# A hybrid decoder layer on one core: the opening's norm weight, the order at the stage entries, and the place of the mLSTM gates

## The chip, the cores and the metric

The kernel runs on one core of a Trainium2 chip, as one launch. The core has a matrix engine (PE; PEld in the profile is its weight load), a vector engine (DVE), a scalar engine (ACT), GpSimd (POOL) and a sync engine (SP) that here only issues DMAs. Each engine works through its own queue in order and waits on semaphores; 16 DMA engines move data between HBM and SBUF. The metric is the device time of one execution in microseconds (us), the median of several runs.

## What is computed

One layer, for 512 tokens of 1024 float32 values: a half-step SwiGLU FFN, a mixer, and a second half-step FFN, each with a norm before and a norm after it.

```python
f = swiglu(rmsnorm(x, ffn1_pre_g[l]), ffn1_w_gate[l], ffn1_w_up[l], ffn1_w_down[l])
x = x + 0.5 * rmsnorm(f, ffn1_post_g[l])
y = hybrid_mixer(rmsnorm(x, mix_pre_g[l]), positions, w_in[l], ...)
x = x + rmsnorm(y, mix_post_g[l])
f = swiglu(rmsnorm(x, ffn2_pre_g[l]), ffn2_w_gate[l], ffn2_w_up[l], ffn2_w_down[l])
x = x + 0.5 * rmsnorm(f, ffn2_post_g[l])
```

`rmsnorm(x, g)` is `x * rsqrt(mean(x*x) + 1e-6) * g`. The mixer joins dilated attention (four heads, three groups each) with an mLSTM of four heads. The mLSTM's gates are, per head and token, `ig = i_pre + i_bias` and `lf = log_sigmoid(f_pre + f_bias)`; running sums of `lf` and a running maximum over them scale its keys and values.

## The kernel before

**Numbers.** Every float32 operand of a projection is split into a rounded high part and the rest, the low part (names with `h` and `l`). A product is three matmuls: high·high, high weight with low activation, and low weight with high activation. ACT makes the high part (a copy into the rounded type), DVE the low part (a subtraction).

**Tiling.** Tokens stand in four tiles of 128 (`xs[0]` to `xs[3]`, D = 1024 values a row). After a norm a tile is turned by eight PE transposes (`turn_norm`) into `hTh` and `hTl`, which hold the model dimension on partitions in eight chunks `k` (KD = 8). Weights come as 512 KB tiles of 128 x 1024 through `load_w` (L79): SP issues the DMA, ACT casts (L86), DVE subtracts (L88).

**Order.** The framework orders each engine's instructions by a planner, which goes by program order and by its own estimate of when each is ready; it may draw a later instruction ahead of one that it takes to be late. `tc.issue_after(i)` ties an instruction behind `i` on its engine. The class `Order` (L243) uses it to write an engine's order out by hand: each of its instructions stands behind the one before. PSUM has eight banks, handed out in turn.

**The opening** (L640 to L661). PE runs 28 matmuls on zeros (L71, `WARM`) while nothing else is there. SP issues x tile 0, then the norm weight `ffn1_pre_g` broadcast to all 128 partitions (`gain`, L91), x tile 1, two weight tiles (gate and up of block f = 0), and x tiles 2 and 3. `prenorm_first` (L134) squares a tile with its row sums on ACT (L138), adds EPS on DVE (L139), takes the power −0.5 on POOL (L100), and multiplies x, the row's factor and the gain in two halves on DVE (L142). Tiles 0 and 1 are turned at once; turning tiles 2 and 3 is put into the list `todo`.

**Stage entries.** `by_halves` (L181) starts a stage before all tokens are ready: first half the tokens (tiles 0 and 1), then the other half, for two groups of two outputs (`b` = 0 and 1, in FFN 1 gate and up). In each group three terms `i` run over both outputs, eight matmuls of 256 columns for each: `i` = 0 high·high, 1 high weight with `hTl`, 2 low weight with `hTh`. After (n, i) = (0, 2) and (1, 0) of the first half one entry of `todo` is run, which turns tile 2 and tile 3. The function is used at three places: FFN 1, the mixer (its first four q/k projections, L899) and FFN 2. At the two later places the weights after the first are cast behind `pins`, the turning of the tiles before.

**FFN rest.** `token_parts` (L251) forms sums of the token halves on DVE and ACT for the later blocks, in a part of `aT`, the tile that receives the FFN's hidden values.

**Mixer.** Attention goes head by head (L954 to L965): q/k projections (`qk_proj`), the exchange of softmax statistics between groups (`exchange`, small steps on DVE and ACT, ending in L841), the transposes of the weights (`turn`, L850), the values. `v12_proj` projects the values of two heads at a time and sends them through DRAM on POOL's queue. `gates()` (L920) turns the gates' pre-activations, applies biases and the logarithm on ACT, and forms two scans and their sums on DVE; `gates_turn` (L940) turns the results for later use by the mLSTM. `gates()` stands behind `scores(0)`, and `gates_turn` in the round of head 1. The mLSTM reads the results only after head 3. The row of the head norm, `hg`, is fetched by POOL into a buffer that `gates()` uses, so it waits for it.

## Time and profile before

| what | value |
|---|---|
| median of 3 runs | 1358.43 us (1358.39 to 1358.49) |
| the profiled execution | 1358.6 us, its span 1356.8 us |
| mean granted PE clock over the span | 0.998 |
| DVE, ACT, POOL busy | 71%, 44%, 2% of the span |
| HBM read and written | 144.63 MB and 4.19 MB, 110 GB/s over the span |

The span runs from the first to the last instruction that the profiler saw; the execution's time has a little more around it. A row of the timeline gives start and duration in us, the engine, the line of the kernel, the operation, what it writes and reads, and the count of instructions merged; in brackets stands how long the engine was idle before it and what ended that. A matmul's duration is longer than the distance to the next start, since they are pipelined. A row of the windows view gives a stretch, its length, the busy time of PE, PEld, DVE, ACT and POOL (each with its count of instructions), PE's granted clock, the share of time in which the 16 DMA engines were busy, and GB/s.

### The profile page before, as it was taken

The page shows a single profiled execution, that of the slowest core. Times are in us where ns is not written, and L with a number is a line of the kernel's source. Part 1 is how long each engine was busy: PE and PEld are TensorE (multiplying, and loading weights), DVE is VectorE, ACT ScalarE, POOL GpSimd, SP SyncE. Part 2 cuts the span into 40 slices and gives each one's busy share as a digit, 9 for nine tenths or more (in the row PEclk, how much of TensorE's full clock was granted, in tenths as well). Part 3 has the DMA queues.
Part 4 walks back from the last instruction along what each step waited for, and adds up shares of the span by engine and source line. Part 5 has one row for each costly group of instructions (what it writes and reads, how often), then busy time and mean ns, then how long its engine had stood idle before and what let it go on. Part 6 is the DMA issues. An engine that isn't in the chain of part 4 may idle for free.

```text
span 1356.8 us, 19908 instructions
## 1 busy us (share of the span) xinstructions
PE 1342.3 (99%) x7976; PEld 1192.8 (88%) x7976; DVE 967.8 (71%) x1482; ACT 601.7 (44%) x969; POOL 32.8 (2%) x56
## 2 busy tenths in 40 slices
PE   8999999999999999999999999999999999999998
PEld 8899999878898888888888888888889999998786
DVE  7799898996772885775756754334378798997983
ACT  5444444554633532445535443222264444444552
POOL 1000000000200000000000000000010000000000
PEclk9999999999999999999999999999999999999999
DMA  5233333654233422422222232233213333335541
GB/s 202 93 109 103 106 104 109 232 174 152 66 95 118 140 82 89 144 74 78 78 78 78 79 117 73 102 97 109 93 46 111 94 97 107 108 106 196 173 148 62
DMA packets 41661, 150.11 MB, mean 111 GB/s; under 512 B 4716, under 2 KB 4716, under 8 KB 41312
## 3 DMA queue, kind: packets, MB, share of 16 engines
q1 hardware_dynamic: 39600, 141.08, 31.7%
q0 software_dynamic: 1968, 7.76, 1.8%
q8 instruction: 62, 1.02, 0.3%
q14 instruction: 31, 0.25, 0.1%
HBM read 144.63 MB, written 4.19 MB: 110 GB/s over the span
## 4 chain that ended last, share of the span: by engine, by line
PE 89%; DVE 6%; ACT 2%; issue 2%; DMA 1%; SPq 0%; DVEq 0%; POOLq 0%; ACTq 0%
PE p L178 11%; PE qb_b L321 9%; PE qb_a L321 9%; PE pq L178 8%; PE pm L178 6%; PE qa_a L321 4%; PE qa_b L321 4%; PE acc_o L229 3%; PE pvo L997 2%; PE pvo L999 2%; PE pvo L998 2%; PE pg_a L188 2%; PE pg_b L188 2%; PE pq L188 2%; PE pg_b L178 2%; PE pg_a L178 2%
## 5 line engine op out<-in xcount | busy, mean ns | idle before, releaser
L178 PE MATMUL pq<-hTh_mx,wh_qk 128*128 128x512 f32 x160 | 63.2, 395 | 0.0
L178 PE MATMUL pq<-hTl_mx,wh_qk 128*128 128x512 f32 x160 | 62.4, 390 | 0.0
L88 DVE TENSOR_TENSOR wl_qk<-wf_qk,wh_qk 128x1024 fp32r<-128x1024 f32 x24 | 29.3, 1220 | 40.2 <-ACT wh_qk L86 29.9
L178 PE MATMUL pm<-hTh_mx,wh_mqk 128*128 128x512 f32 x128 | 50.3, 393 | 0.0
L997 PE MATMUL pvo<-wh_vo,hTh_mx 128*128 128x512 f32 x128 | 50.2, 392 | 0.0
L178 PE MATMUL pm<-hTl_mx,wh_mqk 128*128 128x512 f32 x128 | 49.9, 390 | 0.0
L178 PE MATMUL p<-hTh_mx,wh_gm 128*128 128x512 f32 x128 | 49.9, 390 | 0.0
L999 PE MATMUL pvo<-wl_vo,hTh_mx 128*128 128x512 f32 x128 | 49.8, 389 | 0.0
L178 PE MATMUL p<-hTl_mx,wh_gm 128*128 128x512 f32 x128 | 49.8, 389 | 0.0
L998 PE MATMUL pvo<-wh_vo,hTl_mx 128*128 128x512 f32 x128 | 49.8, 389 | 0.0
L86 ACT CAST wh_qk<-wf_qk 128x1024 fp32r<-128x1024 f32 x24 | 25.0, 1045 | 54.1 <-PE pw L741 27.3
L1150 DVE SCALAR_TENSOR_TENSOR t<-t,p 128x512 f32<-128x512 f32 x16 | 11.0, 688 | 42.7 <-PE p L178 42.7
L88 DVE TENSOR_TENSOR wl_mqk<-wf_mqk,wh_mqk 128x1024 fp32r<-128x1024 f32 x16 | 19.6, 1222 | 29.7 <-ACT wh_mqk L86 25.3
L178 PE MATMUL pq<-hTh_mx,wl_qk 128*128 128x512 f32 x160 | 39.6, 389 | 0.0
L888 DVE SCALAR_TENSOR_TENSOR z<-pm,cw,z 128x511 f32<-128x511 f32 (+2 forms) x48 | 35.2, 742 | 1.4 <-ACT z L886 0.9
L249 ACT CAST wh_a<-cd_a 128x1024 fp32r<-128x1024 f32 x18 | 18.9, 1049 | 39.0 <-DVE cd_a L249 39.0
L321 PE MATMUL qa_a<-hTl_f,wh_a 128*128 128x256 f32 x144 | 36.1, 283 | 0.0
L321 PE MATMUL qa_b<-hTl_f,wh_b 128*128 128x256 f32 x144 | 36.1, 283 | 0.0
L321 PE MATMUL qa_a<-hTh_f,wh_a 128*128 128x256 f32 x144 | 36.1, 283 | 0.0
L321 PE MATMUL qa_b<-hTh_f,wh_b 128*128 128x256 f32 x144 | 36.1, 283 | 0.0
L249 ACT CAST wh_b<-cd_b 128x1024 fp32r<-128x1024 f32 x18 | 18.9, 1049 | 37.9 <-DVE cd_b L249 37.9
L178 PEld LDWEIGHTS pq<-hTh_mx,wl_qk 128*128 128x128 f32 x160 | 30.0, 188 | 6.2
(679 smaller groups left out, 4396.3 us busy)
## 6 DMA issues: line engine op xcount, KB each, us to landing
wf_qk<-in_wqk SPq DMA_DIRECT2D x24, 512.0 KB, 3.6
B_a<-in_wdq SPq DMA_DIRECT2D x21, 512.0 KB, 3.8
B_b<-in_wdq SPq DMA_DIRECT2D x21, 512.0 KB, 4.4
g_a<-in_wgu SPq DMA_DIRECT2D x18, 512.0 KB, 3.7
u_a<-in_wgu SPq DMA_DIRECT2D x18, 512.0 KB, 3.8
g_b<-in_wgu SPq DMA_DIRECT2D x18, 512.0 KB, 3.8
u_b<-in_wgu SPq DMA_DIRECT2D x18, 512.0 KB, 3.8
wf_mqk<-in_wmqk SPq DMA_DIRECT2D x16, 512.0 KB, 3.3
```

The lines of the kernel that those rows point to most:

```text
L86: nc.scalar.copy(wh, wf)
L88: nc.vector.tensor_tensor(wl, wf, wh.bitcast(F32), op=ALU.subtract)
L178: nc.tensor.matmul(out, lhsT=wt[:, k * P:(k + 1) * P], rhs=x[:, k, tok], start=n == 0, stop=n == len(terms) - 1)
L188: nc.tensor.matmul(outs[b][:, tok], lhsT=ws_[b][w][:, k * P:(k + 1) * P], rhs=x[:, k, tok], start=i + k + hf == 0, stop=hf == 1 and i == 2 ...
L229: nc.tensor.matmul(out, lhsT=x[:, tk], rhs=w[:, cs], start=first and n == 0, stop=last and n == 2, skip_group_check=True)
L249: self.last[eng] = getattr(getattr(nc, eng), fn)(*args, **kw).ins
L321: nc.tensor.matmul(out, lhsT=wt[:, i * P:(i + 1) * P], rhs=y[:, i, :], start=first and n == 0, stop=last and n == len(terms) - 1, skip_gro ...
L888: nc.vector.scalar_tensor_tensor(z[:, s:], src[:, :T - s], cw[:, ct, 3 - s:4 - s], z[:, s:], op0=ALU.mult, op1=ALU.add)
L997: nc.tensor.matmul(out, lhsT=hTh[:, k, tk], rhs=wh[:, cs], start=k == 0, stop=False)
L998: nc.tensor.matmul(out, lhsT=hTl[:, k, tk], rhs=wh[:, cs], start=False, stop=False)
L999: nc.tensor.matmul(out, lhsT=hTh[:, k, tk], rhs=wl[:, cs], start=False, stop=k == KD - 1)
L1150: nc.vector.scalar_tensor_tensor(t1[:, b, :], t1[:, b, :], 1.0, p2[b], op0=ALU.add, op1=ALU.mult)
```

## The change

1. The row `ffn1_pre_g` is fetched four times, to partitions 0, 32, 64 and 96 of a tile that DVE has set to zero, by DMAs of 4 KB on ACT's queue; two stream shuffles spread each over its 32 partitions. The broadcast on SP's queue goes.
2. The first weights are loaded into a part of `aT` that is not yet in use (`raw`), before x tiles 2 and 3, and not into buffers of `wf`.
3. The opening's ACT and DVE instructions have a written order (`Order`); tile 1's EPS step stands between the two halves of tile 0's scaling, and tiles 2 and 3 are scaled between and behind the low halves of the first weights. `token_parts` is tied behind the last of them on DVE.
4. The matmuls on zeros are 32 at the start, 8 behind the turning of tile 0, and 5 behind that of tile 1.
5. In `by_halves` the first group of the first half runs terms 0 and 1 of output 0 before those of output 1, at all three places.
6. `gates()` and the fetch of `hg` move into the round of head 2, ahead of the second `v12_proj`; `gates_turn` moves to the round of head 3.

```diff
@@ -32,7 +32,7 @@
 KEEP = 4
 WMAX = 1024
 EARLY = 2
-WARM = 28
+WARM = (32, 8, 5)
 FLUSH = ((0, 2), (1, 0))
 
 
@@ -68,8 +68,11 @@
     warm = act.tile([P, 512], BF16, tag="junk", bufs=1, name="warm")[:, 0:256]
     nc.vector.memset(warm, 0.0)
     wbank = bank("warm")
-    for i in range(WARM):
-        nc.tensor.matmul(wbank[:, 0:256], lhsT=warm[:, 0:P], rhs=warm, start=True, stop=True)
+
+    def fill(n):
+        for i in range(n):
+            nc.tensor.matmul(wbank[:, 0:256], lhsT=warm[:, 0:P], rhs=warm, start=True, stop=True)
+
     ident = ids.tile([P, P], F32, name="ident")
     make_identity(nc, ident)
 
@@ -131,17 +134,6 @@
         nc.scalar.mul(h[:, BANKS[1]], h[:, BANKS[1]], r)
         return h
 
-    def prenorm_first(t, g, where, after=None):
-        h = scratch(f"h_f1{t}", *where)
...
     def turn_norm(t, h, hTh, hTl, name):
         pt = pair(f"pt_{name}{t}")
         dst = slice(t * P, (t + 1) * P)
@@ -182,13 +174,17 @@
         for hf in range(2):
             tok = slice(hf * T // 2, (hf + 1) * T // 2)
             for n, (outs, ws_) in enumerate(groups):
-                for i, (w, x) in enumerate(((0, hTh), (0, hTl), (1, hTh))):
-                    for b in range(2):
-                        for k in range(KD):
-                            nc.tensor.matmul(outs[b][:, tok], lhsT=ws_[b][w][:, k * P:(k + 1) * P], rhs=x[:, k, tok],
-                                             start=i + k + hf == 0, stop=hf == 1 and i == 2 and k == KD - 1,
-                                             skip_group_check=True)
-                    if hf == 0 and (n, i) in FLUSH:
+                terms = ((0, hTh), (0, hTl), (1, hTh))
+                order = [(i, b) for i in range(3) for b in range(2)]
+                if n == 0 and hf == 0:
+                    order[1:3] = order[2:0:-1]
+                for i, b in order:
+                    w, x = terms[i]
+                    for k in range(KD):
+                        nc.tensor.matmul(outs[b][:, tok], lhsT=ws_[b][w][:, k * P:(k + 1) * P], rhs=x[:, k, tok],
+                                         start=i + k + hf == 0, stop=hf == 1 and i == 2 and k == KD - 1,
+                                         skip_group_check=True)
+                    if hf == 0 and b and (n, i) in FLUSH:
                         flush(todo)
 
     def new_hT(name):
@@ -248,6 +244,8 @@
             with tc.issue_after(self.last[eng]) if eng in self.last else nullcontext():
                 self.last[eng] = getattr(getattr(nc, eng), fn)(*args, **kw).ins
 
+    opened = []
+
     def token_parts(low, tmp, hTh, hTl, name):
         def quad(t, i, j):
             return t[:, 4 * i:4 * i + 4, j * H:(j + 1) * H]
@@ -255,8 +253,9 @@
         hf, xs_ = tmp[:, 0:8, :], tmp[:, 8:16, :]
         for j in (1, 0):
             for i in (1, 0):
-                nc.vector.tensor_tensor(quad(hf, i, j), quad(hTh, i, j).bitcast(F32), quad(hTl, i, j).bitcast(F32),
-                                        op=ADD)
+                with tc.issue_after(opened[0]):
+                    nc.vector.tensor_tensor(quad(hf, i, j), quad(hTh, i, j).bitcast(F32),
+                                            quad(hTl, i, j).bitcast(F32), op=ADD)
...
@@ -577,9 +576,9 @@
                 self.product(STEPS[n])
                 self.middle(STEPS[n])
 
-    def ffn(pool, todo, first_w, hT, wgu, wdq, wd, post, finish, name, begin=None, pins=()):
+    def ffn(pool, todo, first_w, hT, wgu, wdq, wd, post, finish, name, begin=None, pins=(), aT=None):
         hTh, hTl = hT
-        aT = pool.tile([P, NF, T], F32, name=f"aT_{name}")
+        aT = aT or pool.tile([P, NF, T], F32, name=f"aT_{name}")
...
@@ -645,21 +644,96 @@
         def load_x(t):
             nc.sync.dma_start(xs[t], a["x"][t * P:(t + 1) * P, :])
 
+        g_pre = work.tile([P, D], F32, tag="gain", bufs=2, name="g_f1pre")
+        rows4 = work.tile([P, D], F32, tag="gain", bufs=2, name="f1pre_rows")
+        nc.vector.memset(rows4, 0.0)
+        for i in range(0, P, 32):
+            nc.scalar.dma_start(rows4[i:i + 1, :], a["ffn1_pre_g"].rearrange("(o d) -> o d", o=1))
         load_x(0)
-        g_pre = gain(a["ffn1_pre_g"], "f1pre", eng=nc.sync)
         load_x(1)
+        aT1 = fa.tile([P, NF, T], F32, name="aT_a")
+        raw = [aT1[:, 2 * b:2 * b + 2, :].rearrange("p a b -> p (a b)") for b in range(2)]
+        for b in range(2):
+            nc.sync.dma_start(raw[b], a["wgu1"][0, :, b * 1024:(b + 1) * 1024])
+        for t in range(2, NT):
+            load_x(t)
+        fill(WARM[0])
+        do = Order()
+        for c in BANKS:
+            do("vector", "stream_shuffle", g_pre[:, c], rows4[:, c], [0] * 32)
         hT1 = new_hT("f1")
-        for t in range(2):
-            h = prenorm_first(t, g_pre, (hbuf + tbuf)[t])
-            pins = turn_norm(t, h, *hT1, "f1")
-            turned = pins[0]
-        first_w = [load_w(a["wgu1"][0, :, b * 1024:(b + 1) * 1024], f"agu0{b}", after=pins if b else ()) for b in range(2)]
+        hs = [scratch(f"h_f1{t}", *(hbuf + tbuf)[t]) for t in range(NT)]
+        rs = {}
+        tt = lambda *args: do("vector", "tensor_tensor", *args[:3], op=args[3])
+
+        def opening_square(t):
+            ss = small.tile([P, 2], F32, tag="ss", name=f"s1_{t}")[:, 0:1]
+            do("scalar", "activation", hs[t], xs[t], AF.Square, scale=D ** -0.5, accum_out=ss)
+            return ss
+
+        def opening_power(t, ss):
+            do("vector", "tensor_scalar", ss, ss, EPS, None, op0=ALU.add)
+            rs[t] = rsqrt(ss, 1, f"f1{t}")
+
+        def opening_scale(t, b):
+            c = BANKS[b]
+            do("vector", "scalar_tensor_tensor", hs[t][:, c], xs[t][:, c], rs[t], g_pre[:, c], op0=MUL, op1=MUL)
+
+        def opening_turn(t):
+            pt = pair(f"pt_f1{t}")
+            for b in range(2):
+                for k in range(4):
+                    i = nc.tensor.transpose(pt[b][:, k * P:(k + 1) * P], hs[t][:, (4 * b + k) * P:(4 * b + k + 1) * P],
+                                            ident)
+            with tc.issue_after(i.ins):
+                fill(WARM[1 + t])
+            return [(pt[b].rearrange("p (k c) -> p k c", c=P), slice(4 * b, 4 * b + 4), slice(t * P, (t + 1) * P))
+                    for b in range(2)]
+
+        def opening_high(src, ks, dst):
+            do("scalar", "copy", hT1[0][:, ks, dst], src)
+
+        def opening_cast(b):
+            wh = wpool.tile([P, WMAX], F32R, tag="wh", bufs=5, name=f"wh_agu0{b}")
+            do("scalar", "copy", wh, raw[b])
+            return wh
+
+        def opening_low(b, wh):
+            wl = wpool.tile([P, WMAX], F32R, tag="wl", bufs=5, name=f"wl_agu0{b}")
+            tt(wl, raw[b], wh.bitcast(F32), SUB)
+            return wh, wl
+
+        ss = [opening_square(t) for t in range(2)]
+        opening_power(0, ss[0])
+        opening_scale(0, 0)
+        opening_power(1, ss[1])
+        for t, b in ((0, 1), (1, 0), (1, 1)):
+            opening_scale(t, b)
+        turned = opening_turn(0)
+        opening_high(*turned[0])
+        whs = [opening_cast(0)]
+        opening_high(*turned[1])
+        turned += opening_turn(1)
+        for x in turned[2:]:
+            opening_high(*x)
+        whs.append(opening_cast(1))
+        pins = (do.last["scalar"],)
+        for i in (0, 2, 1, 3):
+            src, ks, dst = turned[i]
+            tt(hT1[1][:, ks, dst], src, hT1[0][:, ks, dst].bitcast(F32), SUB)
+        ss += [opening_square(2), opening_square(3)]
+        first_w = [opening_low(0, whs[0])]
+        opening_power(2, ss[2])
+        for b in range(2):
+            opening_scale(2, b)
+        first_w.append(opening_low(1, whs[1]))
+        opening_power(3, ss[3])
+        for b in range(2):
+            opening_scale(3, b)
+        opened.append(do.last["vector"])
         todo = []
         for t in range(2, NT):
-            load_x(t)
-        for t in range(2, NT):
-            h = prenorm_first(t, g_pre, (hbuf + tbuf)[t], turned)
-            todo.append(lambda t=t, h=h: turn_norm(t, h, *hT1, "f1"))
+            todo.append(lambda t=t: turn_norm(t, hs[t], *hT1, "f1"))
         gains = []
 
         def load_gains():
@@ -678,7 +752,7 @@
             todo.append(lambda: turn_norm(t, h, *hT, "mx"))
 
         op_ctx.close()
-        pins = ffn(fa, todo, first_w, hT1, a["wgu1"], a["wdq1"], a["wd1"], post1, finish1, "a", begin=load_gains)
+        pins = ffn(fa, todo, first_w, hT1, a["wgu1"], a["wdq1"], a["wd1"], post1, finish1, "a", begin=load_gains, aT=aT1)
     hTh, hTl = hT
 
 
@@ -944,23 +1018,23 @@
             nc.tensor.transpose(ptg[:, 16 + sb * 4:20 + sb * 4], Fc[:, sb * P:(sb + 1) * P], ident[0:4, 0:4])
         nc.vector.tensor_copy(cT, ptg[:, 0:32])
 
-    gates()
     nc.gpsimd.dma_start(selr[:, 0:512], a["sel"])
     caus = mix.tile([P, 1, P], F32, name="caus")
     with tc.issue_after(mixer_from):
         nc.gpsimd.dma_start(caus[:, 0, :], a["caus"])
-    hg = work.tile([P, 1, D], F32, tag="gain", bufs=2, name="hg")
-    nc.gpsimd.dma_start(hg[:, 0, :], a["mlstm_head_g"].partition_broadcast(P))
     for h in range(1, HEADS):
         qk_proj(h, 0)
         exchange(h - 1, sm, val)
         qk_proj(h, 1)
         pT = turn(h - 1, sm)
-        if h == 1:
+        if h == 3:
             gates_turn()
         qk_proj(h, 2)
         values(h - 1, pT, v12)
         if h == 2:
+            gates()
+            hg = work.tile([P, 1, D], F32, tag="gain", bufs=2, name="hg")
+            nc.gpsimd.dma_start(hg[:, 0, :], a["mlstm_head_g"].partition_broadcast(P))
             v12 = v12_proj(1)
         sm, val = scores(h)
     pqs = [m_qk_proj(0, 0)]
```

More of the change, by code (lines that the diff above doesn't have):

```diff
@@ L132, in prenorm @@
         return h
-    def prenorm_first(t, g, where, after=None):
-        h = scratch(f"h_f1{t}", *where)
-        ss = small.tile([P, 2], F32, tag="ss", name=f"s1_{t}")[:, 0:1]
-        with tc.issue_after(after) if after else nullcontext():
-            nc.scalar.activation(h, xs[t], AF.Square, scale=D ** -0.5, accum_out=ss)
-        nc.vector.tensor_scalar(ss, ss, EPS, None, op0=ALU.add)
-        r = rsqrt(ss, 1, f"f1{t}")
-        for c in BANKS:
-            nc.vector.scalar_tensor_tensor(h[:, c], xs[t][:, c], r, g[:, c], op0=ALU.mult, op1=ALU.mult)
-        return h
     def turn_norm(t, h, hTh, hTl, name):
```

## The prediction

> **What bounds the kernel now.** I read the page first: the span and the busy line.
>
> ```profile
> span 1356.8 us, 19908 instructions
> PE 1342.3 (99%) x7976; PEld 1192.8 (88%) x7976; DVE 967.8 (71%) x1482; ACT 601.7 (44%) x969; POOL 32.8 (2%) x56
> ```
>
> PE is busy for all but 14.5 us. An edit that leaves PE's matmuls as they are can gain only where PE waits, or where it runs slowly while it counts as busy. So the second view is that of PE's own waits; each row gives the total, the number of times and the longest. I quote those that the change can reach.
>
> ```profile
> PE pt_f L150 <- DVE h_f L142: 1.4, 1, 1.4
> PE pt_f L150 <- ACT wh_agu L86: 1.3, 1, 1.3
> PE pt L850 <- DVE sm L841: 0.8, 1, 0.8
> PE pq L188 <- ACT wh_qk L86: 0.5, 1, 0.5
> PE pg_b L188 <- ACT wh_bgu L86: 0.5, 1, 0.5
> ```
>
> There are four places: the opening, head 0's transposes (L850), and the first matmuls of the mixer (pq) and of the second FFN (pg_b). The timeline gives the opening:
>
> ```profile
> 1.18 0.42 SPq L93 DMA_DIRECT2D g_f1pre<-in_ffn_pre_g  x1
> 6.33 0.15 DVE L139 TENSOR_SCALAR s<-s 128x1 f32<-128x1 f32 x1 [5.31 <-ACT h_f L138]
> 7.15 1.41 DVE L142 SCALAR_TENSOR_TENSOR h_f<-x,r_f,g_f1pre 128x512 f32<-128x512 f32 x2 [0.67 <-POOL r_f L100]
> 7.70 1.06 ACT L138 ACTIVATE h_f<-x 128x1024 f32<-128x1024 f32 x1 [1.41 <-DMA x<-in_x]
> 9.70 1.41 DVE L142 SCALAR_TENSOR_TENSOR h_f<-x,r_f,g_f1pre 128x512 f32<-128x512 f32 x2 [0.67 <-POOL r_f L100]
> 10.47 2.04 ACT L153 CAST hTh_f<-pt_f 128x512 fp32r<-128x512 f32 x4
> 11.09 2.48 DVE L154 TENSOR_TENSOR hTl_f<-pt_f,hTh_f 128x512 fp32r<-128x512 f32 x4
> 12.08 1.65 PE L188 MATMUL pg_a<-hTh_f,wh_agu 128*128 128x256 f32 x8 [0.25 <-ACT hTh_f L153]
> 13.49 2.35 DVE L88 TENSOR_TENSOR wl_agu<-wf_agu,wh_agu 128x1024 fp32r<-128x1024 f32 x2
> 13.53 0.63 PE L188 MATMUL pg_a<-hTl_f,wh_agu 128*128 128x256 f32 x2
> 17.53 2.08 PE L188 MATMUL pg_a<-hTh_f,wl_agu 128*128 128x256 f32 x16
> 20.24 2.15 PE L188 MATMUL pg_a<-hTh_f,wh_agu 128*128 128x256 f32 x16
> ```
>
> The second token tile lands only at 7.70, because the 512 KB gain broadcast stands between the two x tiles; its normalised rows end at 11.11 (9.70 + 1.41), and the stage starts at 12.08. From 12.08 to 17.53 PE runs 32 matmuls. The chain of waits shows the same form later, at its usual pace:
>
> ```profile
> 19.61 0.87 PE pt_f L150 x8
> 20.48 1.91 PE pg_a L188 x16
> ```
>
> That is 0.12 us a matmul (0.11 a transpose), so 3.84 us for 32, where the opening needs 5.45. The lost **1.61 us** is hidden inside "busy". The windows show why (the ninth figure of a row, before the DMA share, is PE's granted clock):
>
> ```profile
> 12.00:13.00 1.00, 0.92 (x6) 0.92 (x7) 1.00 (x3) 1.00 (x3) 0.00 (x0) 0.83 1.00 410
> 13.00:14.00 1.00, 1.00 (x7) 1.00 (x7) 1.00 (x2) 1.00 (x2) 0.00 (x0) 0.50 0.39 156
> 16.00:17.00 1.00, 1.00 (x10) 1.00 (x9) 1.00 (x1) 0.48 (x1) 1.00 (x1) 0.96 0.89 283
> ```
>
> The clock was full at first, fell to 0.50 after the idle stretches before 12 us, and came back just after 16 us.
>
> **The stage entries.** by_halves now runs, in its first group and half, the gate's high·high and low·high terms before it touches the second weight.
>
> ```profile
> 356.94 0.68 DVE L154 TENSOR_TENSOR hTl_mx<-pt_mx,hTh_mx 128x512 fp32r<-128x512 f32 x1
> 357.74 1.11 PE L188 MATMUL pq<-hTh_mx,wh_qk 128*128 128x256 f32 x8
> 358.31 1.03 ACT L86 CAST wh_qk<-wf_qk 128x1024 fp32r<-128x1024 f32 x1
> 359.39 1.22 PE L188 MATMUL pq<-hTh_mx,wh_qk 128*128 128x256 f32 x8 [0.55 <-ACT wh_qk L86]
> 1007.22 1.11 PE L188 MATMUL pg_b<-hTh_f,wh_bgu 128*128 128x256 f32 x8
> 1008.84 1.22 PE L188 MATMUL pg_b<-hTh_f,wh_bgu 128*128 128x256 f32 x8 [0.51 <-ACT wh_bgu L86]
> ```
>
> In the mixer eight matmuls should take 0.96, yet the next eight start 1.65 later: 0.69 is the wait for the second weight's cast, which ends at 359.34. The low rows are done at 357.62, before the first matmul. So eight low·high matmuls fill 358.70 to 359.66, and the cast is in time with 0.3 to spare. In the second FFN 1.62 − 0.96 = 0.66 goes the same way. What comes next is pulled forward by as much; a start later than these would show as a new wait on h_mx, and I cost it at nothing. **−0.69 and −0.66.** Bounds: −1.35 together if both vanish, 0 if the planner puts the old order back.
>
> **The gates.** The group at L924 to L938 moves from behind scores(0) to the front of the second v12 projection.
>
> ```profile
> 459.02 0.67 DVE L936 TENSOR_TENSOR Gl<-gc,selr 4x512 fp32r<-4x512 f32 x1
> 460.23 0.15 DVE L829 TENSOR_TENSOR ee<-val,mm 128x8 f32<-128x8 f32 x1
> 466.62 2.21 PE L850 MATMUL pt<-ident,sm 128*128 128x128 f32 x15 [0.77 <-DVE sm L841]
> 530.00:535.00 5.00, 5.00 (x23) 4.14 (x23) 1.23 (x1) 1.05 (x1) 0.00 (x0) 1.00 0.13 16
> ```
>
> Today the gates run between head 0's softmax steps on DVE; the step at L829 gets its turn only after L936, and PE waits 0.77 for the last of them. Without the gates that chain is several us earlier, so **−0.77**. PE's eight transposes cost the same at either place. At the new place the windows show DVE busy 1.23 and ACT 1.05 of 5 us, over about 20 us, so the gates' ten DVE operations (about 7 us, if L936's 0.67 stands for each) lie beside matmuls. The cover would fail only if a weight cast came late, which costs at most one cast, 1.05. The head gain's DMA waits for the gates on POOL, and the v12 store is queued behind it; that store waits for the end of the projection anyway. Cost: nothing.
>
> **The opening.** The broadcast (row at 1.18) leaves SP, so x1 and the two weights each move up one 512 KB place. In its place come a memset, four one-row DMAs on ACT's queue and two shuffles, all ahead of tile 0's norm in DVE's written order. Nearest rows:
>
> ```profile
> 0.84 0.17 DVE L69 MEMSET warm<- 128x128 uint32 x1 [0.84 <-PEq L1267]
> 0.95 0.06 DVE L77 MEMSET nhalf<- 128x4 f32 x1
> 1.06 5.54 PE L72 MATMUL warm<-warm 128*128 128x256 bf16 x28 [1.06 <-DVE nhalf L77]
> ...
> L724 DVE STREAM_SHUFFLE sw<-qk x24: 710/717/731, 378.0 to 587.5; 32x512 f32<-32x512 f32 x24
> ...
> out<-x SPq DMA_DIRECT2D x8, 256.0 KB, 2.0
> ...
> selr<-in_sel POOLq DMA_DIRECT2D x1, 8.0 KB, 4.7
> ```
>
> Memset: 124 more words cost 0.11, so 1024 cost about 1.0; it ends near 2.1. Then ACT issues four rows; no row shows an issue on ACT, so I take 0.36 each, between none and SP's 0.42, until 3.6. Landing is 2.0 (SP's row, also a hardware queue) to 4.7 (POOL's row); I take 2.0, so 5.6. The Trainium skill ("DMA: Bandwidth & Descriptors", Anatomy of one DMA) gives about 2.0 us fixed per DMA whatever its size; the row of 256 KB in 2.0 agrees, and the sum would be the same. Shuffles: 2 × 0.72, until 7.05.
>
> Tile 0's first scaling then starts 0.82 later (6.33 to 7.15 today, through POOL) at 7.87; the four scalings in the new order, with tile 1's EPS step between, end at 10.67 (four of 0.65 to 0.70, and 0.1). That is **0.44 before** today's 11.11: x1 now comes in time, and the shuffles use up part of it.
>
> PE: tile 0's last four transposes end at 9.84, eight fills take 0.96 (at 0.12), tile 1's transposes 0.87, five fills 0.60: the stage starts at 12.27, **+0.19**. ACT is no later: tile 1's high copies end at 11.85 and 12.40, since one weight cast of 1.05 now stands among them.
>
> If the clock stays full, the 1.61 is saved. Two waits give some back. (1) The gate's low·high matmuls need four low copies: the second starts at 11.9, the last ends at 13.85 (0.62 to 0.65 each), so half of the eight wait 0.33, until 13.9, and end at 14.38. (2) 24 more matmuls reach the second weight's low half at 17.26. In DVE's written order that half comes behind the first low half (15.05), EPS and POOL (15.9) and tile 2's scalings (17.3): it is done at **18.5**. PE would stand for 1.2 us. Ready by then are tile 2's eight transposes (0.87) and the next group's first matmuls. The planner orders PE by what it takes to be ready, so I expect the transposes and a few matmuls to be drawn forward.
>
> So the last eight matmuls run 18.5 to 19.46, with the transposes and two matmuls (0.24) already done; today that point is 20.24. 19.46 − 0.24 = 19.22: **−1.02**. Bounds: +0.1 with nothing drawn forward (19.46 + 0.87 = 20.33), −1.6 with all waits covered.
>
> Fewer waits for buffers of wf, and x parts behind the opening, lie beside matmuls that do not stall until 60 us: nothing.
>
> **Sum:** −0.69 − 0.66 − 0.77 − 1.02 = −3.14. The profiled execution took 1358.6 (span 1356.8 and 1.8 around it), 0.2 above the median 1358.43. On the median: **1355.3 us**.
>
> The clock is the largest single term. The Trainium skill ("TensorE: Matmul & The Clock Gate", Part 1 and Part 4) says that the clock halves after about one idle window of 3.4 us, and that transposes do not count as activity. The trace agrees as far as it goes: it fell although PE had turned tiles 0 and 1 before 12.08. By that rule the fills, which leave no gap over 2.8 us, keep the clock full.
>
> **Rivals.**
> 1. *Nothing is drawn forward.* PE stands 1.2 us at the second low half, and the clock's gain is lost there: opening +0.1, so 1356.4. For: the written DVE order. Against: today two low·high matmuls (13.53) already stand ahead of the second weight's. Chance 0.22.
> 2. *The clock falls anyway.* PE then needs 1.6 more, most of which the wait for the low half swallows; the group ends at 19.55: 1356.5. For: today it fell with work in that stretch. Chance 0.13.
> 3. *The gain rows come late (slower).* They queue behind x and the weights on the same 16 DMA engines. The stage starts about 6.4 after they land; counting the clock as kept, the opening only breaks even near 6.9, the whole kernel near 8.0. With POOL's 4.7 they land at 8.3; behind the second weight, at 9.5, the stage starts at 15.9 and the clock falls too: +3.8 − 2.1, 1360.1. For: DMA share 1.0 until 13 us. Against: 2.0 for SP's row. Chance 0.10.
> 4. *The entries don't do what they say*, because the planner restores the old order: 1.35 back, 1356.6. Chance 0.05.
> 5. *All waits covered, or rows earlier*: 1354.6. Chance 0.10.
>
> My forecast has the rest, 0.40, and by itself 1354.8 to 1355.8.
>
> **Range and chances.** Rivals 1, 2 and 4 end by 1356.6, the milder half of 3 near 1357.3: the range is 1354.2 to 1357.3. A measurement of this kernel can tell about 0.2%, 2.7 us: faster means below 1355.7. Faster: most of the forecast and all of 5, 0.48; slower 0.05; same 0.47.
>
> **What would show it.** Clock 1.00 from 6 us on (rival 2 if not). The shuffles at about 5.6 (rival 3 if after 8). PE's wait on wl_agu after 17 us: under 0.4 here, 1.2 in rival 1. No wait for wh_qk and wh_bgu, none at L850, none in the second v12 projection. I am wrong if PE shows a new wait past 60 us, which I count at nothing.

## The result, and the profile after

The changed kernel takes **1360.36 us** (median of 22 runs, 1359.15 to 1361.56), the kernel before 1358.12 (22 runs, 1357.69 to 1359.62): ratio 1.0015, 95% interval 1.0009 to 1.0022. The forecast was 1355.3, its range ended at 1357.3. The profiled execution took 1360.38, and 1358.6 of it is the span (1356.8 before). The page of after, span and busy time:

```profile
span 1358.6 us, 19952 instructions
...
PE 1342.9 (99%) x7993; PEld 1194.1 (88%) x7993; DVE 971.1 (71%) x1487; ACT 602.1 (44%) x969; POOL 33.1 (2%) x56
```

PE's busy time is 0.6 longer, so the other 1.2 us of the span is added waiting. PE's waits of after (total, times, longest) say where:

```profile
PE pt_f L686 <- DVE s L245: 5.9, 1, 5.9
...
PE pg_a L184 <- DVE s L245: 0.4, 1, 0.4
```

The waits at head 0's transposes and at the two later entries, 0.8, 0.5 and 0.5 before, have no row left: that part of the change does what it says. One wait of 5.9 us has come in, in the opening, ahead of the first transposes (the two there before were 1.4 and 1.3). The 0.4 stands ahead of the last eight matmuls of the stage's first group, at 24.06 in the timeline below; the forecast expected a wait under 0.4 there. The chain of waits, in order of time (start, length), shows what it is made of:

```profile
0.74 3.69 DMA x<-in_x
...
4.45 5.56 DMA f1pre_rows<-in_ffn_pre_g
...
10.12 1.35 DVE g_f1pre L245 x2
...
13.07 1.94 PE pt_f L686 x8
15.01 1.61 PE warm L74 x8
...
25.39 1.91 PE pg_a L184 x16
```

The chain goes through the fourth row of the norm weight: issued at 4.45, landed at 10.01. My forecast had all four landed at 5.6. The last row is the stage's second group, which stood at 20.48 in the chain of before: **4.91 us late**. The timeline of after, first the opening, then head 0's transposes and the second FFN's entry:

```profile
1.06 6.13 PE L74 MATMUL warm<-warm 128*128 128x256 bf16 x32 [1.06 <-DVE warm L69]
...
2.12 2.54 ACTq L651 DMA_DIRECT2D f1pre_rows<-in_ffn_pre_g  x4
...
4.69 1.28 ACT L245 ACT_TABLE_LOAD   x1 [4.69 <-DMA x<-in_x]
...
10.12 0.72 DVE L245 STREAM_SHUFFLE g_f1pre<-f1pre_rows 128x512 f32<-128x512 f32 x1
...
12.17 0.75 DVE L245 SCALAR_TENSOR_TENSOR h_f<-x,r_f,g_f1pre 128x512 f32<-128x512 f32 x1 [0.67 <-POOL r_f L103]
...
14.09 1.41 DVE L245 SCALAR_TENSOR_TENSOR h_f<-x,r_f,g_f1pre 128x512 f32<-128x512 f32 x2 [0.45 <-POOL r_f L103]
...
14.80 1.81 PE L74 MATMUL warm<-warm 128*128 128x256 bf16 x8
...
16.45 1.04 PE L686 MATMUL pt_f<-ident,h_f 128*128 128x128 f32 x8
...
17.79 1.19 PE L184 MATMUL pg_a<-hTh_f,wh_agu 128*128 128x256 f32 x8
...
22.75 0.93 PE L142 MATMUL pt_f<-ident,h_f 128*128 128x128 f32 x7
...
24.06 1.22 PE L184 MATMUL pg_a<-hTh_f,wl_agu 128*128 128x256 f32 x8 [0.39 <-DVE s L245]
...
25.14 2.04 PE L184 MATMUL pg_a<-hTh_f,wh_agu 128*128 128x256 f32 x15
...
468.94 1.80 PE L924 MATMUL pt<-ident,sm 128*128 128x128 f32 x15
...
1010.92 1.12 PE L184 MATMUL pg_b<-hTl_f,wh_bgu 128*128 128x256 f32 x8
...
1011.88 1.12 PE L184 MATMUL pg_b<-hTh_f,wh_bgu 128*128 128x256 f32 x8
```

Read it against the forecast: shuffles at 10.12 (5.6), first scaling 12.17 (7.87), stage start 17.79 (12.27). The windows show PE's granted clock (ninth figure) falling on the way:

```profile
2.00:3.00 1.00, 1.00 (x7) 0.67 (x6) 0.09 (x1) 0.00 (x0) 0.00 (x0) 1.00 0.84 270
...
6.00:7.00 1.00, 1.00 (x10) 0.77 (x8) 0.00 (x0) 1.00 (x2) 0.00 (x0) 1.00 0.84 221
...
9.00:10.00 1.00, 0.00 (x0) 0.00 (x0) 0.00 (x0) 0.00 (x0) 0.00 (x0) 0.78 1.02 414
10.00:13.00 3.00, 0.00 (x0) 0.00 (x0) 2.22 (x8) 0.00 (x0) 0.55 (x1) 0.50 1.03 421
13.00:16.00 3.00, 2.93 (x14) 2.60 (x15) 2.55 (x4) 1.81 (x3) 0.99 (x1) 0.50 0.59 236
16.00:17.00 1.00, 1.00 (x10) 0.88 (x8) 0.10 (x1) 0.21 (x1) 0.00 (x0) 0.81 0.00 0
17.00:18.00 1.00, 1.00 (x12) 0.94 (x11) 0.29 (x1) 0.91 (x2) 0.00 (x0) 1.00 0.00 0
```

The trace has the clock at half from 9.56 to 16.39. Tile 0's transposes (13.07, 1.94 for eight) and the eight fills from 14.80 run at half clock; tile 1's transposes (16.45, 1.04 for eight), the five fills and the stage's own matmuls, from 17.79, do not.

One thing in this view misleads. The two rows before 7 us both show 1.00, but the trace's first record of the clock begins at 6.15. Until then the fills start 0.21 us apart, as the eight do at half clock, and from then on 0.11. So PE ran slowly at the start, and the prediction's "the clock was full at first" is a misreading; none of its terms rests on it.

To see what each place is worth I took the first start of each run of PE matmuls on one tile, in both traces, and subtracted. The running difference (one profiled execution against one) is +4.91 at the second group of the first FFN, +4.10 after the mixer's entry, +2.74 after `gates_turn` at its new place, +1.98 after the second FFN's entry, and +1.75 at the end. So:

| place | forecast | measured |
|---|---|---|
| opening | −1.02 | +4.91 |
| mixer's entry | −0.69 | −0.81 |
| gates, head 0's transposes | −0.77 | −1.36 |
| second FFN's entry | −0.66 | −0.76 |
| outputs at the end | 0 | −0.23 |
| span | −3.14 | +1.75 |

### The profile page after: what moved, and what is told of

Same layout as the page of the kernel before. It is cut to its first block, busy times and chain, and to the rows that moved or that the text cites. A ratio compares the mean times of both kernels' runs of the same rounds, so it can differ in the third digit from the quotient of the medians.

```text
span 1358.6 us, 19952 instructions
## 1 busy us (share of the span) xinstructions
PE 1342.9 (99%) x7993; PEld 1194.1 (88%) x7993; DVE 971.1 (71%) x1487; ACT 602.1 (44%) x969; POOL 33.1 (2%) x56
## 3 DMA queue, kind: packets, MB, share of 16 engines
q8 instruction: 62, 1.02, 0.3%
## 4 chain that ended last, share of the span: by engine, by line
PE 89%; DVE 6%; ACT 2%; issue 2%; DMA 1%; POOL 0%; DVEq 0%; POOLq 0%; ACTq 0%
PE p L170 11%; PE qb_b L320 9%; PE qb_a L320 9%; PE pq L170 8%; PE pm L170 6%; PE qa_b L320 4%; PE qa_a L320 4%; PE acc_o L225 3%; PE pvo L1071 2%; PE pvo L1073 2%; PE pvo L1072 2%; PE pq L184 2%; PE pg_b L184 2%; PE pg_a L170 2%; PE pg_b L170 2%
```

## The experiments

Three theories for the late rows. **A**: their packets stand behind the 512 KB loads that SP issues, on the same DMA engines. **B**: the fourth row was issued late. In the trace its issue on ACT starts at 4.45 and the third's at 2.90: each DMA takes the next of eight completion semaphores, and the fourth row drew that of x tile 0, which landed at 4.43. **C**: a DMA issued by ACT is slow to start whatever lies ahead. Landing times in this section are the completion-semaphore events of each trace; times of the kernel are medians, with the ratio to the kernel before on the same chip. "Opening" is the difference to before at the first FFN's second group, as in the table; it comes from one profiled execution of each kernel.

**1. The four rows by one DMA on SP, between x tile 1 and the weights**

```diff
-        for i in range(0, P, 32):
-            nc.scalar.dma_start(rows4[i:i + 1, :], a["ffn1_pre_g"].rearrange("(o d) -> o d", o=1))
         load_x(0)
         load_x(1)
+        nc.sync.dma_start(rows4[0:P:32, :], a["ffn1_pre_g"].partition_broadcast(4))
```

> The changed kernel, but the four rows of the norm weight are fetched by one DMA on SP's queue, between x tile 1 and the first weight, instead of four DMAs on ACT's queue. Theory A (the rows' 4 KB packets queued behind the weights' 512 KB on the same 16 DMA engines): with the weights issued after them the rows land near 6 us, the shuffles start there, the stage starts 3.5 to 4 us earlier than in the changed kernel (13.5 to 14.5 instead of 17.8), and the time is 1354.5 to 1356.5. Theory B (the fourth row waited for one of eight reused DMA semaphores and so was issued late): with one DMA there is no reuse by a fourth row, so the same gain; this run doesn't tell A from B. Theory C (a DMA issued by ACT is slow to start, whatever lies ahead): same again, since SP issues it. Against all three: if the rows still land after 8 us, what delays them is x itself, and the time stays near 1360.

Measured: 1357.81, ratio 0.9994 (0.9986 to 1.0003); opening +3.21. Timeline:

```profile
7.88 0.01 DVE L245 LOAD_MASK_SELECT g_f1pre<-f1pre_rows  x1 [5.79 <-DMA f1pre_rows<-in_ffn_pre_g]
```

Some 2.5 less than the changed kernel, but the shuffles start at 7.9 and not near 6, and the time lies above the 1354.5 to 1356.5 expected: all three theories missed the size. Three rows landed at 5.42, 5.54 and 5.72, as A has it, and the fourth at 7.77. Runs 9 and 10 take that up.

**2. The four rows by one DMA on ACT**

```diff
-        for i in range(0, P, 32):
-            nc.scalar.dma_start(rows4[i:i + 1, :], a["ffn1_pre_g"].rearrange("(o d) -> o d", o=1))
+        nc.scalar.dma_start(rows4[0:P:32, :], a["ffn1_pre_g"].partition_broadcast(4))
```

> The changed kernel, but one DMA on ACT's queue fetches all four rows (one issue near 2.1 us, one semaphore) instead of four DMAs of a row each. Theory A (packets behind the weights' bytes): the rows were issued at 2.1 and their first packet moves only when the engines' turn comes, at 5.8 to 8.5; landing 6.5 to 8.6, stage start 14.3 to 16.5, time 1356.5 to 1359. Theory B (semaphore reuse and four issues in a row): landing at most 6.5, as the first row of the changed kernel (6.49), stage start near 14.3, time about 1356.8. Theory C (ACT's queue starts slowly): as the first row, 6.5 or so. A landing of 8 or later speaks for A alone.

Measured: 1359.49, ratio 1.0004 (0.9995 to 1.0013); the rows landed at 7.40, 8.24, 8.59 and 8.84, opening +4.22. Timeline:

```profile
8.97 0.72 DVE L245 STREAM_SHUFFLE g_f1pre<-f1pre_rows 128x512 f32<-128x512 f32 x1
```

One issue at 2.12 and one semaphore, yet far from 6.5: B is not the main cause. The shuffles come 1.15 earlier here than in the changed kernel, and B can hardly explain more than that; part of it may be chance, since run 7, which fetches the rows just as the changed kernel does, has them 0.71 earlier too. Landing and time are a little above the ranges given for A (8.6 and 1359).

**3. The old opening with the new entries and gates**

```diff
+                if n == 0 and hf == 0:
+                    order[1:3] = order[2:0:-1]
...
-    gates()
...
-        if h == 1:
+        if h == 3:
             gates_turn()
...
         if h == 2:
+            gates()
...
```

> The kernel before with two of the change's three parts: the order at the stage entries, and the gates, their turning and the head norm's DMA moved to heads 2 and 3. The opening (broadcast by SP, 28 matmuls on zeros, the planner's order) is the old one. My theory: PE's starts fall behind those of the kernel before by 0.8 us after the mixer's entry, 1.4 more by the second v12 projection and gates_turn, 0.8 more at the second FFN's entry: sum -2.9, time about 1355.2 (0.9978 of before). By the prediction's own terms (0.69, 0.66, 0.77): -2.1, 1356.0. Rival (the gains in the changed kernel's trace are partly slack given back by its late opening): the sum is under 1.5. In the first FFN's entry the new order also applies to the old opening: 0 to -0.5, since the clock is low there.

Measured: **1355.37**, ratio 0.9976 (0.9966 to 0.9986). The running difference is +0.1 after the opening, −0.70 after the mixer's entry, −2.08 after `gates_turn`, −2.84 after the second FFN's entry, −2.91 at the end. The three gains stand by themselves; none was slack handed back by a late opening.

**4. The changed kernel with the old broadcast**

```diff
-        rows4 = work.tile([P, D], F32, tag="gain", bufs=2, name="f1pre_rows")
-        nc.vector.memset(rows4, 0.0)
-        for i in range(0, P, 32):
-            nc.scalar.dma_start(rows4[i:i + 1, :], a["ffn1_pre_g"].rearrange("(o d) -> o d", o=1))
         load_x(0)
+        nc.sync.dma_start(g_pre, a["ffn1_pre_g"].partition_broadcast(P))
         load_x(1)
...
-        for c in BANKS:
-            do("vector", "stream_shuffle", g_pre[:, c], rows4[:, c], [0] * 32)
```

> The changed kernel with the norm weight fetched as before the change: one broadcast to 128 partitions by SP between x tile 0 and x tile 1, with no rows, no clearing and no shuffles. The written engine order, the fills of 8 and 5 matmuls, the raw loads, the entries and the gates stay as changed. My theory (the rows' landing is the whole loss): the gain is there by 6 to 7 us, x tile 1 lands near 7.7 as before, tile 1's scalings end near 11, the stage starts at 12.2 to 12.8 with the clock full, and the second low half is at 18 to 18.5: opening -0.5 to -1.2 against before, time 1354 to 1355. Rival (the written order of DVE and ACT costs by itself, whatever the rows do): opening 0 to +1.5, time 1355.5 to 1357.

Measured: **1354.58**, ratio 0.9970 (0.9959 to 0.9981), the lowest ratio of the study; opening −1.05. Timeline:

```profile
6.40 0.75 DVE L245 SCALAR_TENSOR_TENSOR h_f<-x,r_f,g_f1pre 128x512 f32<-128x512 f32 x1 [0.67 <-POOL r_f L103]
...
11.96 1.20 PE L184 MATMUL pg_a<-hTh_f,wh_agu 128*128 128x256 f32 x8
...
16.84 0.93 PE L142 MATMUL pt_f<-ident,h_f 128*128 128x128 f32 x7
...
18.11 1.22 PE L184 MATMUL pg_a<-hTh_f,wl_agu 128*128 128x256 f32 x8 [0.34 <-DVE wl_agu L245]
```

This is the opening as forecast from the stage's start on: matmuls from 11.96 (forecast 12.27) at full clock (its mean over the run is 1.000), tile 2's transposes drawn forward, a wait of 0.34 for the second weight's low half. So the rest of the opening's change (written order, fills, loads into `aT`, order of the first group) is worth a full microsecond together, and the rows, with their clearing and shuffles, turn it into a loss of 4.91. What each part of that microsecond is worth was not separated.

**5. SP's loads behind x tile 1 held back until the shuffles are done**

```diff
...
         for c in BANKS:
             do("vector", "stream_shuffle", g_pre[:, c], rows4[:, c], [0] * 32)
+        for b in range(2):
+            do("vector", "memset", raw[b][:, 0:4], 0.0)
+        for b in range(2):
+            held[0] = nc.sync.dma_start(raw[b], a["wgu1"][0, :, b * 1024:(b + 1) * 1024]).ins
...
```

> The changed kernel with its four row DMAs on ACT, but SP's weights and x tiles 2 and 3 are held back until the shuffles are done (four values of each weight's place are cleared on DVE behind the shuffles, and SP's loads follow that), so that only x tiles 0 and 1, 1 MB, lie ahead of the rows. The time means nothing here (the weights come late): 1361 to 1365. What is read is the landing of the rows. Theory A (packets behind the weights' bytes): rows 1 to 3 land by 6.0 to 6.5 instead of 6.5, 8.6 and 9.1, the fourth, whose DMA semaphore is that of x tile 0, about 2 after its issue at 4.45, at 6.5; shuffles at 6.5 instead of 10.1. Theory C (ACT's queue slow by itself): landing as in the changed kernel, shuffles after 9. Theory B (the fourth row's late issue alone): first three rows as in the changed kernel, 6.5, 8.6 and 9.1.

**6. x tiles 0 and 1 held back too**

```diff
+        for t in range(2):
+            do("vector", "memset", xs[t][:, 0:4], 0.0)
...
+        for t in range(2):
+            load_x(t)
...
```

> As the run with the weights held back, but x tiles 0 and 1 are held behind the shuffles too: the four row DMAs on ACT are the only transfers on the chip until they have landed. This measures the 2.0 of my forecast by itself; the time means nothing (everything comes late, 1364 to 1370). If 2.0 is what such a DMA takes when nothing lies ahead, the first row lands near 4.6 (issue 2.1 to 2.6) and the fourth near 5.5, so the shuffles start at 5.5, as forecast. If a row of 4 KB takes 3 or more by itself, the shuffles start at 6.5 or later, and the forecast would have been wrong on an empty machine too.

SP's other loads are tied behind these. Both changes leave ACT's four row DMAs as they are. The timelines, of run 5 and then of run 6:

```profile
2.12 1.34 ACTq L654 DMA_DIRECT2D f1pre_rows<-in_ffn_pre_g  x4
...
3.49 1.28 ACT L248 ACT_TABLE_LOAD   x1 [3.49 <-issue]
...
6.76 0.01 DVE L248 LOAD_MASK_SELECT g_f1pre<-f1pre_rows  x1 [4.67 <-DMA f1pre_rows<-in_ffn_pre_g]
...
14.40 1.23 PE L187 MATMUL pg_a<-hTh_f,wh_agu 128*128 128x256 f32 x8 [0.92 <-ACT hTh_f L248]
```

```profile
2.12 1.34 ACTq L654 DMA_DIRECT2D f1pre_rows<-in_ffn_pre_g  x4
...
4.81 0.01 DVE L248 LOAD_MASK_SELECT g_f1pre<-f1pre_rows  x1 [2.73 <-DMA f1pre_rows<-in_ffn_pre_g]
```

Same engine, same four DMAs, issued from 2.12 on; only what lies ahead differs:

| ahead of the rows, on the same DMA engines | rows landed | shuffles |
|---|---|---|
| nothing (run 6) | 3.55, 4.00, 4.39, 4.68 | 4.84 |
| x tiles 0 and 1, 1 MB (run 5) | 6.08, 6.27, 6.45, 6.63 | 6.79 |
| x tiles and weights (after) | 6.49, 8.62, 9.10, 10.01 | 10.12 |

With fewer DMAs in flight, the fourth row's issue does not wait in runs 5 and 6 (3.19 instead of 4.45), so these runs take B away too. The second and third rows make the clean comparison: they were issued at 2.66 and 2.90 in all three. That is A, and C falls: alone, ACT's rows land 1.3 to 1.5 after the start of their issue. With x ahead, the rows land just after x tile 1's last share (5.89). My expectation of run 5's time missed widely: 1356.99 (one run) instead of 1361 to 1365. The weights came 6.5 later to the queue, but the first was on chip by 12.25, while tile 1's transposes ran from 11.78, and PE waited only 0.92. The loads that held up the rows were not needed so early. Run 6 took 1361.89 (one run, expected 1364 to 1370).

**7. The changed kernel with 68 matmuls on zeros at the start**

```diff
-WARM = (32, 8, 5)
+WARM = (68, 8, 5)
```

> The changed kernel with 68 instead of 32 matmuls on zeros at the start, so that PE has work until about 11 instead of 7.2 while the rows are on their way; nothing else differs. This separates the clock's share of the loss from the landing's. Theory (the half clock from 9.9 to 16.8 is a cost of its own, on the transposes and the fills of 8 and 5): the clock stays full, tile 0's transposes, the fills and tile 1's transposes take half as long, the stage starts at 16.0 to 16.6 instead of 17.8, the next group at 23.4 to 24.0 instead of 25.1, time 1358.8 to 1359.4 against 1360.3. Rival (DVE's scalings, which end at 15.5, hold the stage anyway): stage start 17.3 or later, time within 0.4 of 1360.3.

Measured: 1358.22, ratio 0.9999 (0.9990 to 1.0008); opening +2.82, stage start 15.81. Windows:

```profile
10.00:13.00 3.00, 0.67 (x6) 0.42 (x5) 2.27 (x7) 0.00 (x0) 1.19 (x2) 1.00 1.02 418
13.00:16.00 3.00, 3.00 (x26) 2.72 (x27) 2.39 (x4) 2.97 (x5) 0.35 (x1) 1.00 0.61 238
```

Against the same windows of after: clock 1.00 for 0.50, 26 instructions on PE for 14 in the three us from 13. The gain of 2.1 is more than I expected. In the profiled execution (1358.17) 0.71 of it is that the rows came earlier (shuffles 9.41 for 10.12); whether they did in the other ten is not known. Timeline:

```profile
9.41 0.72 DVE L245 STREAM_SHUFFLE g_f1pre<-f1pre_rows 128x512 f32<-128x512 f32 x1
...
23.06 2.15 PE L184 MATMUL pg_a<-hTh_f,wh_agu 128*128 128x256 f32 x16
```

From the shuffles to the second group it is 13.65 here (23.06 − 9.41) and 15.02 in after (25.14 − 10.12): **1.37** is the clock's own share, from one execution of each.

**8. Three changes in the written order of run 4**

```diff
-        opening_scale(0, 0)
+        for b in range(2):
+            opening_scale(0, b)
         opening_power(1, ss[1])
...
-        first_w = [opening_low(0, whs[0])]
-        opening_power(2, ss[2])
+        first_w = [opening_low(b, whs[b]) for b in range(2)]
```

The third change, not printed, puts both high copies of tile 0 ahead of the first weight's cast on ACT.

> The kernel with the norm weight broadcast by SP and all else as changed (1354.58), with three places of the written order altered: both scalings of tile 0 ahead of tile 1's EPS step on DVE, both high copies of tile 0 ahead of the first weight's cast on ACT, and the second weight's low half directly behind the first's on DVE, ahead of tile 2's scalings. In the run before, PE waited 1.2 for tile 0's second half (8.35 on DVE, behind an EPS step that waited for x tile 1) and 0.34 for the second low half (18.05). Theory: stage start 11.4 instead of 11.96, no wait for wl_agu, the next group at 18.2 to 18.6 instead of 19.19, time 1353.6 to 1354.0. Rival (tile 1's chain from x tile 1 sets the stage's start): stage start 11.8 to 12.0, only the 0.34 goes, time 1354.2 to 1354.4.

Measured: 1354.57, ratio 0.9975 (0.9965 to 0.9985): no gain over run 4, so both the theory and its rival expected too much. The stage does start earlier (11.63), and the wait for the low half is gone. PE's waits show what took its place:

```profile
PE pt_f L142 <- DVE h_f L245: 0.4, 1, 0.4
```

Tile 2's scaling now stands behind the second low half on DVE, and behind the next weight's low part, which the planner put ahead of it, so tile 2's transposes wait. One wait was traded for another.

**9. One DMA of four rows on SP, between x tiles 0 and 1**

```diff
...
         load_x(0)
-        load_x(1)
+        first = held[0] = nc.sync.dma_start(rows4[0:P:32, :], a["ffn1_pre_g"].partition_broadcast(4)).ins
+        with tc.issue_after(first):
+            load_x(1)
...
```

> The changed kernel, but the four rows are fetched by one DMA on SP's queue, between x tile 0 and x tile 1 (all other loads tied behind it), so that 512 KB lie ahead of them. In the runs so far the shuffles started at 4.8 with nothing ahead of the rows, at 6.8 with x tiles 0 and 1 ahead, at 10.1 with the weights ahead too. Theory A (the bytes ahead): three rows land near 4.5, the fourth (which came 2.1 after the others where SP fetched them behind x tile 1) by 6.6 at the latest; shuffles at 4.6 to 6.7, tile 0's scaling at 7.0 to 8.8, clock full, the opening 0.2 to 1.2 faster than before the change; time 1354.3 to 1355.5. Rival (four rows fetched by one DMA go to four DMA engines, one of which is always about 2 late, wherever the DMA stands): shuffles at 6.5 or later, time 1355.5 to 1357.

**10. Four row DMAs on SP, between x tile 1 and the weights**

```diff
-        for i in range(0, P, 32):
-            nc.scalar.dma_start(rows4[i:i + 1, :], a["ffn1_pre_g"].rearrange("(o d) -> o d", o=1))
         load_x(0)
         load_x(1)
+        for i in range(0, P, 32):
+            nc.sync.dma_start(rows4[i:i + 1, :], a["ffn1_pre_g"].rearrange("(o d) -> o d", o=1))
```

> The changed kernel with its four row DMAs issued by SP, between x tile 1 and the first weight, instead of by ACT. Against the run with one DMA of four rows at the same place (rows at 5.42, 5.54, 5.72 and 7.77) it tells whether the late fourth row was the single DMA's spread over several DMA engines. Theory (single rows go one behind the other on one DMA engine, behind x tile 1's share of it): all four by 6.0 to 6.7, as in the run with the weights held back (6.08 to 6.63), shuffles at 6.2 to 6.9, opening +0.5 to +1.5 against before, time 1355.5 to 1356.7. Rival (any small DMA is overtaken by the weights that follow it): the last row at 7.5 or later, time 1357.5 to 1358.5.

Run 9 drops ACT's row DMAs and ties every other load of SP behind the new one. Measured: run 9 1356.57, ratio 0.9981 (0.9972 to 0.9990), opening −0.30; run 10 1355.60, ratio 0.9979 (0.9970 to 0.9987), opening +1.52. The shuffles in the two timelines, run 9 and then run 10:

```profile
6.30 0.72 DVE L248 STREAM_SHUFFLE g_f1pre<-f1pre_rows 128x512 f32<-128x512 f32 x1
```

```profile
6.83 0.72 DVE L245 STREAM_SHUFFLE g_f1pre<-f1pre_rows 128x512 f32<-128x512 f32 x1
```

In run 9 three rows landed at 4.15, 4.17 and 4.21, the fourth at 6.16: 1.95 after the third, as in run 1 (2.05). In run 10 all four landed evenly, at 5.94, 6.14, 6.40 and 6.67, with the weights behind them. So on SP's queue the straggler came with the single DMA of four rows, at both places tried, and single rows ahead of the weights are not overtaken by them. It does not come with every such DMA: in run 2, on ACT's queue, the four rows landed within 1.44 of each other, the last 0.25 after the third. Why one of the four is late stays open. Run 9's shuffles lie in the range of A, its time in that of the rival; run 10 came out as its theory has it. Run 10 also answers C once more: behind the same 1 MB of x, the last row landed at 6.67 when SP issued it and at 6.63 when ACT did (run 5). Both runs beat the kernel before, neither beats the plain broadcast of run 4.

## Why the prediction was wrong

**The step that failed** is in the opening: "Landing is 2.0 us (SP's row, also a hardware queue) to 4.7 (POOL's row); I take 2.0, so 5.6." The 2.0 came from the output rows, on a queue with nothing ahead. In the opening SP has just put 512 KB loads on the same 16 DMA engines, whose share reads 1.02 and 1.03 from 9 to 13 in the windows of after. There a row took 4.4 to 6.2 from its issue to its landing. Alone, the rows are even faster than I took (shuffles at 4.84 in run 6 for 5.6). x ahead costs 1.95 (run 5), the weights and the fourth row's late issue another 3.33 (after), of which one DMA and one issue takes back 1.15 (run 2). The late issue is a second, smaller miss: I had the four issues done by 3.6, and the fourth ended at 4.66.

The sizes close. The shuffles came 10.12 − 5.6 = 4.52 late, the clock that fell meanwhile cost 1.37 (run 7): 5.89. The opening missed its forecast by 4.91 + 1.02 = 5.93.

**It was rival 3**, which I gave 0.10. Its mechanism is the one shown: stage start 6.4 after the rows (6.40 after the start of the shuffles in runs 7 and 9, where the clock stays full), landing 9.5 (10.0). That its time, 1360.1, comes so near to 1360.36 is luck. It has the opening at +3.8 where +4.91 was measured, since it names the fall of the clock and adds nothing for it, and the other places at −2.1 where −3.16 was measured; the two errors of 1.1 cancel. What I set against it, SP's quiet row, was no evidence about a loaded stretch; the DMA share of 1.0 that I listed for it was. With that row in view the rival's chance should have been large, and the forecast a landing between the two ends.

The Trainium skill, "DMA: Bandwidth & Descriptors" (Queues, rings and completion order), says that SP and ACT each own one ring on each of the same 16 DMA engines, and that an engine takes turns between rings by packets of several descriptors. By that rule another issuing engine brings no free path, and the landings of runs 6, 5 and after are in line with it; the turns themselves no run here shows. I had drawn on the same page for a fixed 2.0 per DMA, from a section on DMAs that GpSimd issues; for these rows it was 1.3 to 1.5 alone (run 6), 3.4 to 4.0 with x ahead (run 5) and 4.4 to 6.2 in after.

**The opening's other steps held**, which run 4 shows with rows out of play: transposes drawn forward and the second low half done at 18.05 (18.5). That its opening, −1.05, is so near to the −1.02 is partly chance, since it reaches the stage by another way: x tile 1 behind the broadcast as before, but no shuffles. Rival 1 is out: in after too, seven of tile 2's transposes stand at 22.75, ahead of the last eight matmuls at 24.06. Rival 2, that the clock falls anyway, did not come up in run 4, where the norm weight is in time and the clock stays full to the end of PE's work. It fell in after because PE had nothing to do from 7.19 to 13.07; run 7 fills that gap and it stays. How much room the forecast had is open: in run 10, with the shuffles at 6.83, the profiled execution's clock fell from 9.47 to 12.89.

**The fills, which I had as a guard, became a cost.** In after the eight fills hold PE from 14.80 until 16.45 at half clock, while tile 1's rows are ready at 15.50 (14.09 + 1.41): its transposes start 0.95 after that. They could not protect the clock here, since the gap that opened was not the one that they fill.

**The entries**: right, 0.12 and 0.10 more than the waits that were counted; no new wait came up. Rival 4 is out.

**The gates**: right in kind, 0.59 too small. I counted the wait of 0.77 ahead of head 0's transposes. But the transposes themselves took 2.21, since they kept pace with DVE's scalings of `sm`, as the timeline of before shows:

```profile
466.21 2.11 DVE L841 TENSOR_SCALAR sm<-sm,w 128x128 f32<-128x128 f32 x8
```

With those done early they take 1.80 (468.94 in after). That is 0.41 more, and what is left of the difference lies in the starts around it (argued from the two traces, not tested by a run of its own). PE shows no wait in the second v12 projection, as expected.

## What to carry to other kernels

Take the landing time of a new DMA from a row in the same stretch, under the same load; here a 4 KB row behind 1 MB and more in flight took 3.4 to 6.2 us instead of 1.3 to 1.5, and the engine that issued it made no difference (last row at 6.63 from ACT and 6.67 from SP, behind the same 1 MB). Before a transfer is made small, ask whether it is the bytes or the place in the queue that costs: here 16 KB in any place that was tried did not beat the 512 KB broadcast in second place. Where a change puts a new operand ahead of everything else in a stage, price its late end first, and give it the chance that the load on that resource suggests.

## What was not expected of the hardware

**Completion semaphores run out.** With eight DMAs in flight in the opening, the fourth row and x tile 3 each waited for an earlier load that had the same one of eight semaphores, and the wait stood in the issuing engine's own queue: ACT's table load came at 4.69, against 3.49 in run 5, where none of the four issues had to wait for an earlier load. The issues themselves, which also wait for the clearing of the rows' tile, cost ACT more: with the row DMAs on SP the load stood at 0.74 (runs 1, 9 and 10).

**The clock moves in steps of 3.41 us**, and a step with some work in it can still count as idle. In after the trace's records of the clock begin at 6.15, 9.56 and 16.39, so 3.41 and 6.83 apart. In after, runs 1, 2 and 10 the step that led to the fall held 1.0 to 1.15 us of fills; in runs 5, 6 and 9 one with 1.6 to 1.8 us kept the clock. Where the steps lie differs between executions: the first record begins anywhere from 3.93 (run 7) to 6.82 (run 4). The Trainium skill, "TensorE: Matmul & The Clock Gate" (Part 1), calls the window free-running; the times agree. Run 10's eleven times lie in two groups, seven at 1355.28 to 1355.68 and four at 1356.60 to 1357.03; run 9's in five at 1355.05 to 1355.70 and six at 1356.57 to 1356.97. The distance of about 1.3 is near the clock's share in run 7. The profiled execution of run 10, where the clock fell, is of its longer group (1356.90), that of run 9, where it stayed, of its shorter one (1355.33), so a step's place fits as the cause; with one profile of each it is argued, not shown.
